# Eleven weight pieces subtracted on the pool engine, and x loaded over two queues, in a three-block fp32 kernel

## The chip, the cores and the metric

The kernel runs on one core of a Trainium2 chip. The metric is device time in microseconds (us) of one execution, the median of several runs. The engines are named as in the profile: PE is TensorE (matrix products), DVE is VectorE, ACT is ScalarE, POOL is GpSimd, and SP is SyncE, which here only issues transfers (DMAs). A DMA can be issued from the queue of SP, ACT or POOL.

## The reference

Three different blocks run one after the other on x, 512 tokens of 1,024 channels in fp32. Each one normalizes x, mixes tokens with two to four mixers, multiplies the merged result with an output matrix and adds it to x, normalizes again and adds an FFN. The first block, cut to this frame:

```python
def conv_glu_ffn(h, w_up, conv_w, w_down):
    u = causal_dwconv(h @ w_up.astype(h.dtype), conv_w)
    gate, up = jnp.split(u, 2, axis=-1)
    return (jax.nn.silu(gate) * up) @ w_down.astype(h.dtype)

def first_block(x, ...):
    ...
        h = rms_norm(x, mix_norm[l])
        z = h @ w_in[l].astype(h.dtype)
        ...
        merged = jnp.sum(gates.astype(ys.dtype) * ys, axis=2)
        x = x + merged @ w_o[l].astype(h.dtype)
        h2 = rms_norm(x, ffn_norm[l])
        x = x + conv_glu_ffn(h2, ffn_up[l], ffn_conv[l], ffn_down[l])
    return x

def reference(...):
    x = first_block(x, ...)
    x = second_block(x, ...)
    return third_block(x, ...)
```

The second block (gated delta rule and RWKV mixers) and the third (GLA and SSM mixers) have the same frame, with shift, scale and gate vectors from a condition (a "modulation").

## The kernel before

**Layout.** x lies as 8 tiles of 128 channels by 512 tokens. Work on x around a normalization is done in two halves of 256 tokens, so much of it has the shape 128x256. Weights are cut into blocks of 128x128; 8 blocks make a piece of 128x1024 fp32 (512 KB), and there are 464 pieces.

**Weights.** `load` (L319 to L331) issues the DMA of a raw piece `wr` from SP (L325), copies it on ACT to `wh` in a shorter form, fp32r (L328), and lets DVE form the rest `wl = wr - wh` (L329). Inputs are split the same way into `h` tiles. Each product then takes three matmuls: wh times high part, wh times low part, wl times high part (L358 to L360 in halves, L372 to L374 over all 512 tokens). `wr`, `wh` and `wl` have 3 buffers each, and `ahead` (L346) loads pieces up to two ahead of the one in use.

**Normalization.** `Rms.add` squares a tile of x on ACT (L495, L498 for the first tile) and adds the square to a sum (L496), on DVE, except for the second half of x at the start, where POOL adds. `stat` sums over channels with small matmuls on PE (L352, eight of them for a half). `mean` and `rsqrt` (L513 to L535) then do a chain of tiny 128x2 steps on DVE, each of which needs the one before it: shift and subtract, and three times L518, L520, L522. `factor` puts the result on a diagonal (L546, DVE) and spreads it over all partitions with one matmul (L548, PE). `into` multiplies x with it (L565, DVE), copies the high part on ACT (L569 or L572) and forms the low part on DVE (L570 or L573). These are the next products' inputs.

**Start.** `begin` (L758) issues the first half of x (8 tiles, L765), the first 256 columns of a constants table `con` (L205), the parameters `par` (L206), the second half of x, and then, in `constants`, the rest of `con` in five chunks (L213). Two constant tiles are copied to fp32r on ACT (L772): `onesr`, from the first 256 columns, and `bd64r`, whose source lies in the first of the five chunks.

**Ends.** `tail` (L816) does the output product of the mixers: five output tiles one by one, the last three (TAIL = 3) together in halves through `lins`, each added to x (L831); then the norm, the FFN, and x plus the FFN (L858, L860). In `ffn` the last output tile is made in halves (L475 to L480). At both ends the next product needs all of x, so the chain of adding, squares, `stat`, `rsqrt`, `factor` and `into` stands between two streams of matmuls.

**Order.** The code gives an order and priorities (`first`, which raises one); a scheduler then orders each engine's queue by priority and its own forecast of times. On the chip every engine works through its queue in that order and waits where an input is not there. `z.run` and `busy` weave background work in between; the change doesn't touch them.

Of the kernel before, what the change touches and what calls it, by code (L numbers as in the profile page):

```python
# [7 lines left out]
F32 = mybir.dt.float32  # L8
# [4 lines left out]
ALU = mybir.AluOpType  # L13
# [5 lines left out]
S = 512  # L19
# [166 lines left out]
class K:  # L186
# [78 lines left out]
                if next(g, self) is self:  # L265
                    gens.remove(g)

    busy = 0

    def tick(self):  # L270
        if not self.busy:
# [13 lines left out]
    def ada(self, which, c, ctx=False, chain=None):  # L285


        n = c.shape[2]
        s, th = [self.new([P, 8, n], tag="adas", bufs=2) for _ in range(2)]
        half = chain.t(8 * n).rearrange("p (k n) -> p k n", n=n)  # L290
        self.V.tensor_scalar(half, c, 0.5, None, op0=ALU.mult)
        self.A.activation(th, half, AF.Tanh)
        self.V.scalar_tensor_tensor(s, th, 1.0, half, op0=ALU.add, op1=ALU.mult)
        out = self.new([P, 64], tag="ada", bufs=1)
        self.ada_out = out
        yield
        for o in range(6):
            acc = [self.tile("ac", 1024) for _ in range(2 if ctx and o < 2 else 1)]
            for k in range(8):
                raw = self.tile("wa", 1024)  # L300
                at = ((which * 6 + o) * 8 + k) * 1024
                self.nc.sync.dma_start(raw, self.ap["wa"][:, at:at + 1024])
                for m, a in enumerate(acc):
                    if k:
                        self.V.scalar_tensor_tensor(a, raw, s[:, k, m:m + 1], a, op0=ALU.mult, op1=ALU.add)  # L305
                    else:
                        self.V.tensor_scalar(a, raw, s[:, k, m:m + 1], None, op0=ALU.mult)
                yield
            ps = self.bank("aux")
            for m, a in enumerate(acc):  # L310
                for b in range(8):
                    self.column(ps[:, 8 * m + b:8 * m + b + 1], a[:, b * P:b * P + P])
            self.V.tensor_copy(out[:, 8 * o:8 * o + 8], ps[:, :8])
            if len(acc) > 1:
                self.V.tensor_copy(out[:, 48 + 8 * o:56 + 8 * o], ps[:, 8:16])
            yield


    def load(self, n):  # L319
        n = min(n, self.ap["w"].shape[0])  # L320
        while self.loaded < n:
            i = self.loaded
            with self.first():
                raw = self.new([P, PIECE * P], F32, tag="wr", bufs=3)
                self.nc.sync.dma_start(raw, self.ap["w"][i])  # L325
                hi = self.new([P, PIECE * P], F32R, tag="wh", bufs=3)
                lo = self.new([P, PIECE * P], F32R, tag="wl", bufs=3)
                self.A.activation(hi, raw, AF.Copy)  # L328
                self.V.tensor_tensor(lo, raw, hi.bitcast(F32), op=ALU.subtract)  # L329
            self.pieces[i] = (hi, lo)  # L330
            self.loaded += 1  # L331

# [111 lines left out]
    def ffn(self, h, up, down, mid, out):  # L444


        m = {}

        def ups(a, b):
            for j in range(a, b):  # L450
                self.busy = 1 if j else self.busy
                if j % 11 == 0:
                    m[j // 11] = [], []
                if j > 1 or UP == 2 and j:
                    g, u = [self.lin(h, *w) for w in up(j)]
                elif j:
                    u = self.lin(h, *up(j)[1])
                    g = g1
                else:
                    (_, ps), _ = self.lins(h, *up(j), *(up(1)[:1] if UP > 2 else ()))  # L460
                    g, u = ps[:2]
                    g1 = ps[-1]
                self.split(m[j // 11], mid(j, g, u), lambda: self.tile("p", dt=F32R))

        ups(0, 11 + FFN_HEAD)
        for o in range(8):
            out(o, self.lin(m[0], down, P * o), slice(0, S))
            self.tick()
        ups(11 + FFN_HEAD, 22)
        for o in range(7):  # L470
            out(o, self.lin(m[1], down, P * o, 11 * P), slice(0, S), True)
            if o == 4:
                self.run(*self.bg)
                self.bg, self.busy = [], 0
        ps = self.bank("mm")  # L475
        w = self.take([(down, 11 * P + P * k, 7 * P) for k in range(11)])
        for n in HALVES:
            self.product(ps, w, m[1], n)
            out(7, ps, n, True)
        self.ahead()  # L480


class Rms:
# [260 lines left out]
def load_x(z, src, tag):  # L744
    X = [z.tile(tag) for _ in range(8)]
    for k in range(8):
        z.nc.gpsimd.dma_start(X[k], src[:, k * S:k * S + S])
    return X
# [9 lines left out]
def begin(z, src, which):  # L758

    with z.phase({"aux": 4}, x=8, f=8, wa=(2, 1024), ac=(3, 1024)):  # L760
        X = [z.tile("x") for _ in range(8)]
        for n in HALVES:
            with z.first((1 if n.start else 3) * HP):
                for k in range(8):
                    z.nc.sync.dma_start(X[k][:, n], src[:, k * S + n.start:k * S + n.stop])  # L765
                if n.start == 0:
                    z.parameters()
            if n.start == 0:
                z.load(1)
        z.constants()  # L770
        for x, y in ((z.onesr, z.ones), (z.bd64r, z.bd64)):
            z.A.activation(x, y, AF.Copy)  # L772
        c = Chain(z, "f", "aux")
        if which > 1:
            z.run(ada(z, which, c))
            modulation(z, which)
        r, h = Rms(c), z.rings()
        z.new([P, 96], tag="pad")
        a, b = HALVES
        for k in range(8):  # L780
            r.add(X[k], k, a)
        with z.first(2 * HP):
            by = r.of(r.mean(a))
            for k in range(8):
                r.add(X[k], k, b, z.G)
            by = r.into(h, X, *norm1(z, which), a, by, r.factor(lambda: r.mean(b)), 4)
            r.into(h, X, *norm1(z, which), b, by)
        return h


def norm1(z, which):
    return (z.q("mix_norm"), None) if which == 1 else (z.mod[:, 8:16], z.mod[:, 0:8])
# [8 lines left out]
def modulation(z, which):  # L801

    V = z.V
    mod = z.new([P, 64], tag=f"mod{which}")
    s = f"_{which}"
    V.tensor_tensor(mod[:, :48], z.ada_out[:, :48], z.q("b_ada" + s), op=ALU.add)
    if which == 3:
        V.tensor_tensor(mod[:, 48:], z.ada_out[:, 48:], z.q("b_ada" + s)[:, :16], op=ALU.add)
    for a, n in ((8, "norm1_w"), (32, "norm2_w"), (56, "norm1_w"))[:which]:
        V.scalar_tensor_tensor(mod[:, a:a + 8], mod[:, a:a + 8], 1.0, z.q(n + s), op0=ALU.add, op1=ALU.mult)  # L810
    for a in (16, 40)[:which - 1]:
        V.tensor_scalar(mod[:, a:a + 8], mod[:, a:a + 8], 0.5, None, op0=ALU.mult)
    z.mod = mod


def tail(z, m, src, dst, which, after):  # L816
# [3 lines left out]
    with z.phase({"aux": 4, "x": 1}, x=8, p=34, f=9, wa=(2, 1024), ac=(2, 1024)):  # L820
        c = Chain(z, "f", "aux")
        X = load_x(z, src, "x")
# [6 lines left out]
        def residual(o, ps, n):  # L829
            g = 0.5 if which == 1 else old[:, 16 + o:17 + o]  # L830
            V.scalar_tensor_tensor(X[o][:, n], ps[:, n], g, X[o][:, n], op0=mult, op1=add)  # L831
            r.add(X[o], o, n)

        w = "w_o" if which == 1 else "w_out" + s
        for o in range(8 - TAIL):
            residual(o, z.lin(m, w, P * o), slice(0, S))
        v = []
        for n, ps in z.lins(m, *((w, P * o) for o in range(8 - TAIL, 8))):
            with z.first(3 * HP):
                for e in range(TAIL):  # L840
                    residual(8 - TAIL + e, ps[e], n)
                v.append(r.mean(n))
                if not n.start:
                    by = r.of(v[0])
        with z.first(3 * HP):
            by = r.into(m, X, *norm, HALVES[0], by, r.factor(v[1]))
            r.into(m, X, *norm, HALVES[1], by)
        h = m

        own = {2: "norm_f_w_2", 3: "final_norm_w_3"}.get(which)  # L850
        r1 = Rms(c) if own else None
# [1251 lines left out]
def whole(z, out, blocks=(1, 2, 3)):  # L2103
    src = z.ap["x"]
    z.mod = None
    h = begin(z, src, blocks[0])
    for n, w in enumerate(blocks):
        m = (first, second, third)[w - 1](z, h)
        last = n == len(blocks) - 1
        dst = out if last else z.new([P, 8 * S], tag=f"x{w}", pool=z.dr)  # L2110
        h = tail(z, m, src, dst, w, None if last else w + 1)
        src = dst
# [20 lines left out]
```

## Time and profile before

| | us |
|---|---|
| median of 3 runs | 3309.65 |
| lowest and highest run | 3306.63, 3312.49 |
| the profiled execution | 3309.27 |
| its span (first to last instruction) | 3307.5 |
| PE busy in the span | 3217.7 (97%) |
| DVE, ACT, POOL busy | 67%, 45%, 3% |

How to read it: the span is what the trace covers; the profiled execution was 1.8 us longer than its span. A busy PE leaves some 90 us in which it does nothing. Those lie at the start and at a few seams between streams of matmuls. A timeline row gives the start in us, the time in us, the engine, the line, the operation with output and input, the shape, and how many instructions the row holds; in square brackets stands how long the engine was idle before, and what ended that wait.

### The profile page before, as it was taken

To read this page: it belongs to the slowest core of one execution; us is meant where nothing else is said; L and a number is where in the kernel's file an instruction comes from. 1 tells how busy PE (TensorE), PEld (TensorE's weight loads), DVE (VectorE), ACT (ScalarE), POOL (GpSimd) and SP (SyncE) were. 2 spreads that over 40 slices of the span, in tenths; PEclk is the share of its full clock that TensorE was granted. 3 is DMA by queue.
4 is the path that set the end of the run, shared out by engine and by line. 5 is a ranking of instruction groups with operands and counts; after the bars stand their busy time and mean duration, and the time that the engine had idled before them with its cause. 6 is when DMAs were issued, how large, how long until landed. Compare 5 with 4: busy or idle time off the path is not lost. (4 is left out here: it accounts for less than half of the span.)

```text
span 3307.5 us, 48313 instructions
## 1 busy us (share of the span) xinstructions
PE 3217.7 (97%) x19041; PEld 2671.8 (81%) x19041; DVE 2232.0 (67%) x3675; ACT 1496.2 (45%) x2493; POOL 101.5 (3%) x186
## 2 busy tenths in 40 slices
PE   7999999999999999999999999999999999999998
PEld 6778888888887787888888878888877778888887
DVE  5696646976577578666886568677688986453344
ACT  6542523433346657653432334645546665232222
POOL 0000000000000000000000001000010001000000
PEclk9999999999999999999999999999999999999999
DMA  4223333764332112215466324213227577423332
GB/s 135 71 71 102 92 124 96 229 203 148 109 101 72 52 39 83 79 43 181 136 208 224 96 82 134 73 64 98 84 87 233 174 218 234 128 90 96 96 97 76
DMA packets 128324, 393.33 MB, mean 119 GB/s; under 512 B 16056, under 2 KB 23480, under 8 KB 128096
## 3 DMA queue, kind: packets, MB, share of 16 engines
q1 hardware_dynamic: 113776, 346.82, 33.8%
q0 software_dynamic: 13168, 42.36, 3.7%
q8 instruction: 150, 2.46, 0.3%
q10 hardware_dynamic: 1152, 1.05, 0.1%
q14 instruction: 78, 0.64, 0.1%
HBM read 358.44 MB, written 31.74 MB: 118 GB/s over the span
## 5 line engine op out<-in xcount | busy, mean ns | idle before, releaser
L373 PE MATMUL mm<-h,wh 128*128 128x512 f32 x2400 | 948.2, 395 | 0.0
L372 PE MATMUL mm<-h,wh 128*128 128x512 f32 x2400 | 945.7, 394 | 1.6 <-ACT t L952 1.5
L374 PE MATMUL mm<-h,wl 128*128 128x512 f32 x2400 | 947.2, 395 | 0.0
L328 ACT ACTIVATE wh<-wr 128x1024 fp32r<-128x1024 f32 x464 | 490.5, 1059 | 935.9 <-PE mm L373 658.7
L329 DVE TENSOR_TENSOR wl<-wr,wh 128x1024 fp32r<-128x1024 f32 x464 | 567.2, 1223 | 459.6 <-ACT wh L328 453.8
L372 PEld LDWEIGHTS mm<-h,wh 128*128 128x128 f32 x2400 | 452.4, 188 | 98.1 <-issue 6.0
L374 PEld LDWEIGHTS mm<-h,wl 128*128 128x128 f32 x2400 | 452.1, 188 | 96.4 <-issue 4.5
L373 PEld LDWEIGHTS mm<-h,wh 128*128 128x128 f32 x2400 | 452.3, 188 | 95.0 <-issue 4.8
L373 PE MATMUL mm<-p,wh 128*128 128x512 f32 x599 | 233.4, 390 | 1.1 <-DVE p L434 1.1
L372 PE MATMUL mm<-p,wh 128*128 128x512 f32 x599 | 233.6, 390 | 0.0
L374 PE MATMUL mm<-p,wl 128*128 128x512 f32 x599 | 233.0, 389 | 0.0
L358 PE MATMUL mm<-h,wh 128*128 128x256 f32 (+1 forms) x480 | 158.5, 342 | 14.6 <-DVE t L1944 5.5
L359 PE MATMUL mm<-h,wh 128*128 128x256 f32 (+1 forms) x480 | 159.1, 337 | 0.6 <-DVE h L573 0.6
L360 PE MATMUL mm<-h,wl 128*128 128x256 f32 (+1 forms) x480 | 157.0, 332 | 0.0
L305 DVE SCALAR_TENSOR_TENSOR ac<-wa,adas,ac 128x1024 f32<-128x1024 f32 x98 | 125.3, 1280 | 24.4 <-DMA wa<-wa 23.9
L373 PEld LDWEIGHTS mm<-p,wh 128*128 128x128 f32 x599 | 112.4, 188 | 25.0 <-DVE p L434 1.7
L372 PEld LDWEIGHTS mm<-p,wh 128*128 128x128 f32 x599 | 112.4, 188 | 23.4
L374 PEld LDWEIGHTS mm<-p,wl 128*128 128x128 f32 x599 | 112.4, 188 | 23.4
L358 PEld LDWEIGHTS mm<-h,wh 128*128 128x128 f32 x480 | 91.2, 195 | 26.1 <-ACT h L572 5.1
L359 PEld LDWEIGHTS mm<-h,wh 128*128 128x128 f32 x480 | 93.4, 196 | 9.8 <-DVE h L573 2.0
L360 PEld LDWEIGHTS mm<-h,wl 128*128 128x128 f32 x480 | 93.4, 196 | 8.4
L754 DVE SCALAR_TENSOR_TENSOR f<-mm,par,f 128x511 f32<-128x511 f32 (+1 forms) x128 | 95.3, 745 | 1.1
(660 smaller groups left out, 5188.3 us busy)
## 6 DMA issues: line engine op xcount, KB each, us to landing
wr<-w SPq DMA_DIRECT2D x464, 512.0 KB, 3.6
wa<-wa SPq DMA_DIRECT2D x96, 512.0 KB, 4.3
e<-cum SPq DMA_DIRECT2D x64, 256.0 KB, 5.4
x<-x POOLq DMA_DIRECT2D x40, 256.0 KB, 5.1
s<-ecum SPq DMA_DIRECT2D x64, 128.0 KB, 4.7
cd<-t POOLq DMA_DIRECT2D x24, 256.0 KB, 2.3
gt<-t POOLq DMA_DIRECT2D x16, 256.0 KB, 2.5
fr<-gt SPq DMA_DIRECT2D x16, 256.0 KB, 2.9
```

The source lines that it names most:

```text
L305: self.V.scalar_tensor_tensor(a, raw, s[:, k, m:m + 1], a, op0=ALU.mult, op1=ALU.add)
L328: self.A.activation(hi, raw, AF.Copy)
L329: self.V.tensor_tensor(lo, raw, hi.bitcast(F32), op=ALU.subtract)
L358: self.T.matmul(ps[:, n], lhsT=wh, rhs=x[0][k][:, n], start=k == 0, stop=False)
L359: self.T.matmul(ps[:, n], lhsT=wh, rhs=x[1][k][:, n], start=False, stop=False)
L360: self.T.matmul(ps[:, n], lhsT=wl, rhs=x[0][k][:, n], start=False, stop=k == last)
L372: self.T.matmul(out, lhsT=wh, rhs=x[0][k], start=k == 0, stop=False)
L373: self.T.matmul(out, lhsT=wh, rhs=x[1][k], start=False, stop=False)
L374: self.T.matmul(out, lhsT=wl, rhs=x[0][k], start=False, stop=k == last)
L754: z.V.scalar_tensor_tensor(out[:, d:], src[:, :S - d], w[:, n - 1 - d:n - d], out[:, d:], op0=ALU.mult, op1=ALU.add)
```

## The change

Two things. First, a flag `edge` is set around the output product of the last three tiles of each mixer end up to and including the normalization behind it, and around the last product of each FFN. While it is set, `load` gives the subtraction of L329 to POOL (`self.G`) in place of DVE (`self.V`). `load` is called for 11 pieces there: three at each of the three mixer ends and one at each of the first two FFN ends (at the third FFN end no piece is left to load). The other 453 stay on DVE. Second, the 16 transfers of x in `begin` go alternately over the queues of SP (even tiles) and ACT (odd tiles), in both halves.

```diff
-    busy = 0
+    busy, edge = 0, False
...
                 self.A.activation(hi, raw, AF.Copy)
-                self.V.tensor_tensor(lo, raw, hi.bitcast(F32), op=ALU.subtract)
+                (self.G if self.edge else self.V).tensor_tensor(lo, raw, hi.bitcast(F32), op=ALU.subtract)
...
         ps = self.bank("mm")
+        self.edge = True
         w = self.take([(down, 11 * P + P * k, 7 * P) for k in range(11)])
         for n in HALVES:
             self.product(ps, w, m[1], n)
             out(7, ps, n, True)
         self.ahead()
+        self.edge = False
...
                 for k in range(8):
-                    z.nc.sync.dma_start(X[k][:, n], src[:, k * S + n.start:k * S + n.stop])
+                    (z.nc.sync, z.nc.scalar)[k % 2].dma_start(X[k][:, n], src[:, k * S + n.start:k * S + n.stop])
...
         v = []
+        z.edge = True
         for n, ps in z.lins(m, *((w, P * o) for o in range(8 - TAIL, 8))):
...
-        h = m
+        h, z.edge = m, False
```

The lines of the changed kernel have higher numbers: L496 becomes L498, L522 becomes L524, L548 becomes L550, L765 becomes L767, L772 becomes L774, L858 becomes L861.

The scheduler orders the queues anew. Three places matter.

The first is SP's queue at the start. `x6` to `x13` are the eight tiles of x, `con` the constants, `par` the parameters, `wr14` and `wr87` the first two raw weight pieces. Before:

```order
L765 DMA x6_73<-x 128x256
L765 DMA x7_74<-x 128x256
L765 DMA x8_75<-x 128x256
L765 DMA x9_76<-x 128x256
L765 DMA x10_77<-x 128x256
L765 DMA x11_78<-x 128x256
L765 DMA x12_79<-x 128x256
L765 DMA x13_80<-x 128x256
L205 DMA con2_64<-con 128x256
L206 DMA par1_63<-par 128x803
L765 DMA x6_73<-x 128x256
L325 DMA wr14_92<-w 128x1024
```

Now:

```order
L767 DMA x6_73<-x 128x256
L767 DMA x8_75<-x 128x256
L205 DMA con2_64<-con 128x256
L767 DMA x10_77<-x 128x256
L206 DMA par1_63<-par 128x803
L767 DMA x12_79<-x 128x256
L767 DMA x6_73<-x 128x256
L325 DMA wr14_92<-w 128x1024
L767 DMA x8_75<-x 128x256
L767 DMA x10_77<-x 128x256
L767 DMA x12_79<-x 128x256
L325 DMA wr87_321<-w 128x1024
```

SP has eight transfers of x fewer; the two halves of each odd tile stand in ACT's queue, one right behind the other, those of `x7`, `x9` and `x11` ahead of ACT's first computation and those of `x13` behind its first square.

The second place is ACT's queue later in the start. `f35` to `f41` are squares of the first half of x and `f48` to `f54` those of the second half, `wh` are weight pieces, `smga` is a small parameter tile. Before:

```order
L495 ACTIVATE f41_150<-x13_80 128x256
L772 ACTIVATE onesr3_65<-con2_64 128x128
L1198 ACTIVATE smga1407_7995<-par1_63 8x1
L498 ACTIVATE f17_113<-x6_73 128x256
L328 ACTIVATE wh15_94<-wr14_92 128x1024
L495 ACTIVATE f48_183<-x7_74 128x256
L495 ACTIVATE f49_186<-x8_75 128x256
L495 ACTIVATE f50_189<-x9_76 128x256
L495 ACTIVATE f51_192<-x10_77 128x256
L495 ACTIVATE f52_195<-x11_78 128x256
L495 ACTIVATE f53_198<-x12_79 128x256
L495 ACTIVATE f54_201<-x13_80 128x256
```

Now:

```order
L328 ACTIVATE wh15_94<-wr14_92 128x1024
L497 ACTIVATE f40_147<-x12_79 128x256
L497 ACTIVATE f41_150<-x13_80 128x256
L1201 ACTIVATE smga1407_7995<-par1_63 8x1
L328 ACTIVATE wh88_323<-wr87_321 128x1024
L328 ACTIVATE wh91_425<-wr90_423 128x1024
L774 ACTIVATE bd64r4_66<-con2_64 128x128
L497 ACTIVATE f48_183<-x7_74 128x256
L497 ACTIVATE f49_186<-x8_75 128x256
L497 ACTIVATE f50_189<-x9_76 128x256
L497 ACTIVATE f51_192<-x10_77 128x256
```

The second-half squares stand behind two more weight pieces (`wh88`, `wh91`), which before came only after them, and behind the copy to `bd64r`, which before stood far behind them, among the copies of L569.

The third place is the end of the first FFN. DVE's queue had the subtraction of the last product's loaded piece, `wl1357`, in the middle of the chain of `rsqrt` steps (`nw`) before:

```order
L518 SCALAR_TENSOR_TENSOR nw1349_7627<-nw1346_7615,nw1348_7626 128x2
L520 TENSOR_TENSOR nw1349_7627<-nw1349_7627,nw1348_7626 128x2
L522 SCALAR_TENSOR_TENSOR nw1348_7626<-nw1349_7627,nw1348_7626 128x2
L329 TENSOR_TENSOR wl1357_7695<-wr1355_7692,wh1356_7694 128x1024
L518 SCALAR_TENSOR_TENSOR nw1349_7627<-nw1346_7615,nw1348_7626 128x2
L520 TENSOR_TENSOR nw1349_7627<-nw1349_7627,nw1348_7626 128x2
L522 SCALAR_TENSOR_TENSOR nw1348_7626<-nw1349_7627,nw1348_7626 128x2
L518 SCALAR_TENSOR_TENSOR nw1349_7627<-nw1346_7615,nw1348_7626 128x2
L520 TENSOR_TENSOR nw1349_7627<-nw1349_7627,nw1348_7626 128x2
L522 SCALAR_TENSOR_TENSOR nw1348_7626<-nw1349_7627,nw1348_7626 128x2
L858 TENSOR_TENSOR x819_4241<-x819_4241,mm1343_7572 128x256
L546 TENSOR_SCALAR f1350_7639<-con2_64,nw1348_7626 128x128 x2
```

In the changed kernel that row is in POOL's queue, and the steps stand in a row in DVE's. On PE the matmul that spreads the factor (`aux1351`) has moved, here as a piece of the difference:

```order
 L360 MATMUL mm1343_7572<-p1285_7166,wl1336_7515 128x256
+L550 MATMUL aux1351_7642<-f1350_7639,con2_64 128x256
 L358 MATMUL mm1343_7572<-p1298_7244,wh1335_7514 128x256
 L359 MATMUL mm1343_7572<-p1299_7245,wh1335_7514 128x256
 L360 MATMUL mm1343_7572<-p1298_7244,wl1336_7515 128x256
-L548 MATMUL aux1351_7642<-f1350_7639,con2_64 128x256
 L352 MATMUL aux1354_7682<-con2_64,f891_4735 32x1 x8
```

It now stands three matmuls earlier, inside the last product (`mm1343`), so that the end of that product waits for it too. At the mixer ends of the second and third block the same matmul has moved nine matmuls forward; at the first mixer end it has not moved.

## Rows read from the trace of the kernel before

**Rows 1.** Busy time by stretch (us): span, then PE, PEld, DVE, ACT, POOL, clock, DMA share.

```profile
0.00:19.68 19.68, 1.93 (x34) 1.12 (x34) 10.57 (x37) 12.36 (x27) 6.33 (x11) 1.00 0.87 281
...
928.00:946.00 18.00, 14.32 (x124) 11.84 (x123) 14.72 (x52) 7.46 (x14) 0.54 (x1) 1.00 0.28 92
...
1950.00:1970.00 20.00, 15.67 (x157) 13.58 (x156) 17.26 (x74) 8.43 (x16) 0.00 (x0) 0.91 0.16 53
```

**Rows 2.** Timeline of PE at the start.

```profile
9.32 0.39 PE L352 MATMUL aux<-con,f 128*32 128x1 f32 x16 [9.32 <-DVE f L496]
...
19.36 0.39 PE L352 MATMUL aux<-con,f 128*32 128x1 f32 x16 [5.45 <-POOL f L496]
19.68 0.58 PE L358 MATMUL mm<-h,wh 128*128 128x256 f32 x1
```

**Rows 3.** Timeline of SP's queue at the start: issues of transfers.

```profile
0.75 3.71 SPq L765 DMA_DIRECT2D x<-x  x8
...
11.26 2.86 SPq L325 DMA_DIRECT2D wr<-w  x3
14.16 2.58 SPq L213 DMA_DIRECT2D con<-con  x5
```

**Rows 4.** Transfers issued up to 22 us: count, KB each, median us to landing.

```profile
con<-con SPq DMA_DIRECT2D x4, 256.0 KB, 6.0
```

**Rows 5.** Timeline of ACT at the start.

```profile
11.27 1.06 ACT L328 ACTIVATE wh<-wr 128x1024 fp32r<-128x1024 f32 x1 [1.10 <-DMA wr<-w]
12.23 1.93 ACT L495 ACTIVATE f<-x 128x256 f32<-128x256 f32 x6
...
21.14 0.29 ACT L772 ACTIVATE bd64r<-con 128x128 fp32r<-128x128 f32 x1
```

**Rows 6.** Timeline of POOL at the start, single instructions.

```profile
12.71 1.64 POOL L496 TENSOR_TENSOR f<-f,f 128x256 f32<-128x256 f32 x1 [12.26 <-ACT f L495]
...
16.04 0.73 POOL L496 TENSOR_TENSOR f<-f,f 128x256 f32<-128x256 f32 x1
```

**Rows 7.** Timeline of DVE at the start, beside those POOL instructions.

```profile
12.55 1.22 DVE L329 TENSOR_TENSOR wl<-wr,wh 128x1024 fp32r<-128x1024 f32 x1
...
16.39 0.66 DVE L570 TENSOR_TENSOR h<-f,h 128x256 fp32r<-128x256 f32 x1
...
19.90 0.42 DVE L570 TENSOR_TENSOR h<-f,h 128x256 fp32r<-128x256 f32 x1
```

**Rows 8.** Timelines of ACT, DVE and PE at the first FFN's end.

```profile
931.29 1.06 ACT L328 ACTIVATE wh<-wr 128x1024 fp32r<-128x1024 f32 x1 [0.90 <-PE mm L359]
...
932.50 0.16 DVE L522 SCALAR_TENSOR_TENSOR nw<-nw,nw 128x2 f32<-128x2 f32 x1
932.61 1.22 DVE L329 TENSOR_TENSOR wl<-wr,wh 128x1024 fp32r<-128x1024 f32 x1
...
935.13 0.48 DVE L546 TENSOR_SCALAR f<-con,nw 128x128 f32<-128x128 f32 x2
...
935.75 0.67 PE L548 MATMUL aux<-f,con 128*128 128x256 f32 x2 [1.15 <-DVE f L546]
937.77 0.31 PE L352 MATMUL aux<-con,f 128*32 128x1 f32 x16 [1.34 <-DVE f L496]
```

**Rows 9.** Timelines of ACT and DVE at the first mixer end.

```profile
561.01 1.06 ACT L328 ACTIVATE wh<-wr 128x1024 fp32r<-128x1024 f32 x1 [2.19 <-issue]
...
563.25 0.42 DVE L496 TENSOR_TENSOR f<-f,f 128x256 f32<-128x256 f32 x1
563.96 0.42 DVE L831 SCALAR_TENSOR_TENSOR x<-x,x 128x256 f32<-128x256 f32 x1 [0.29 <-PE x L360]
```

**Rows 10.** Timelines of ACT and DVE at the second mixer end.

```profile
1577.85 1.06 ACT L328 ACTIVATE wh<-wr 128x1024 fp32r<-128x1024 f32 x1 [2.29 <-PE mm L359]
...
1580.73 1.06 ACT L328 ACTIVATE wh<-wr 128x1024 fp32r<-128x1024 f32 x1 [1.51 <-issue]
...
1578.70 0.16 DVE L520 TENSOR_TENSOR nw<-nw,nw 128x2 f32<-128x2 f32 x1
...
1584.48 0.48 DVE L831 SCALAR_TENSOR_TENSOR x<-x,mod,x 128x256 f32<-128x256 f32 x1 [1.10 <-PE x L360]
```

## Prediction, made before the changed kernel was run

> **What bounds the kernel now.** I read the busy shares first, then the windows around the stretches where PE stands still, then the timelines there. PE works in nearly the whole span, so a cheaper DVE instruction is worth something only where PE waits for DVE. There are three kinds of such places. The first is the start: PE does 1.93 us of work in the first 19.68 us, while the DMA engines are 87% busy [rows 1]. The first product comes at 19.68, behind an L352 that waited 5.45 us for POOL's adds [rows 2]. So the second-half squares and adds set the start, not the first half, whose L352 was done at 9.32. The second kind is the FFN end: PE waits 1.15 us for DVE's L546 and then 1.34 us for L496 [rows 8]. The third is the mixer end, where the last add to x (L831) waits for PE, and not PE for it [rows 9, 10]; PE only waits behind that add, for the norm that follows it.
>
> **The start.** The change takes eight issues off SP. One costs 3.71 / 8 = 0.46 us [rows 3], and the raw piece wr14 is now eighth in SP's queue and was twelfth: it is issued up to 4 x 0.46 = 1.9 us sooner, or no sooner where SP waits for something else. What decides, however, is ACT's new order. There the copy to bd64r stands ahead of all second-half squares. Its source is the first constants chunk, which SP issues right behind three weight transfers, at 14.16 [rows 3]. The third of these comes only after DVE has subtracted the first piece, which ended at 12.55 + 1.22 = 13.77 [rows 7]. The chunk therefore moves with wr14: issue at 12.3 to 14.2. Such a chunk took 6.0 us to land [rows 4], so it is there at 18.3 to 20.2, and with 0.29 us for the copy [rows 5] the squares begin at 18.6 to 20.5; before they began at 12.23 [rows 5]. From there to the L352 it was 19.36 - 12.23 = 7.1 us [rows 2, 5], in which one of the seven adds took 1.64 us and an undisturbed one takes 0.73 [rows 6]. Seven of the latter and a square of some 0.4 us make 5.5 us. The L352 lands at 24.1 to 27.6 where it was at 19.36: **4.7 to 8.3 us later**. I take 5.0, near the early end, since less is queued ahead of the chunk than before. The copy cost nothing before because it ran at 21.14 [rows 5], after the squares; that cover is gone. ACT's own issues of x delay its squares too, by about 0.46 us each, but this lies ahead of the wait for the chunk and adds nothing. What is late next are POOL's adds and, behind the squares on ACT, the copies of L571.
>
> The Trainium skill (DMA: Bandwidth & Descriptors, section Issuing engines are not separate DMA queues) says that transfers issued from several engines run on the same 16 DMA engines, and that the gain is only the sequencer's issue time. By that rule the two queues give at most the 1.9 us above, with the order of the engines unchanged; the 87% agrees with it.
>
> **The FFN ends.** 11 subtractions leave DVE; 453 stay. POOL's time for a 128x1024 subtraction isn't in the trace. Its 128x256 add takes 0.73 us [rows 6]: four times that is 2.9 us, the upper end. DVE went from 0.42 us at 256 [rows 7] to 1.22 at 1024, a factor of 2.9, which gives 2.1 us, the lower end. I take 2.4, since part of 0.73 must be a fixed cost. The other question is what DVE can do meanwhile. At the start POOL's first add took 1.64 us in place of 0.73 while DVE's L329 ran [rows 6, 7], and a DVE L570 took 0.66 in place of 0.42 beside a POOL add that began at 16.04 [rows 6, 7]. In both pairs the later one ended only after the earlier had let go. All of these have two SBUF inputs, as the subtraction and the rsqrt steps have. I read this as a **lock**: while POOL subtracts, such DVE steps stand still.
>
> The Trainium skill (SBUF — State Buffer, section Who interferes with whom) states it as a rule: DVE's second port pair is shared with GpSimd under an exclusive lock. The two pairs agree in size. Without that rule the sum would be the first rival's.
>
> At the first FFN end wh is done at 931.29 + 1.06 = 932.35 [rows 8]. POOL then holds the lock to 934.45 to 935.25 (taken: 934.75). DVE's L522, at 932.50 before, waits for that. From L522 to L546 it was 935.13 - 932.50 = 2.63 us [rows 8], of which about 1.14 was the subtraction and 0.33 the add L858, now behind L546; 1.16 us are left. L546 begins at 935.6 to 936.4 (935.9) and L550, 0.62 us behind as before (935.75 - 935.13), at 936.2 to 937.0. But L550 now stands three matmuls ahead of the product's end, so PE holds the end back: some 0.9 us for it (0.67 before) and those three, then the add to x, a square and the add of the square at 0.4 us each with hand-overs, together 1.4 us. L352 comes at 938.5 to 939.3 where it was at 937.77: 0.7 to 1.5 later, I take **+1.1**. The second FFN end has the same pattern, so 2.2 us for both (1.4 to 3.0). Behind POOL's instruction in its own queue stands one store of x, for which nobody waits soon.
>
> **The mixer ends.** At the first, wh is done at 561.01 + 1.06 = 562.07, POOL holds to 564.2 to 565.0 (564.5). L496, which has two SBUF inputs, ran at 563.25 and the last L831 at 563.96 [rows 9]. Now L496 ends at 564.6 to 565.4 and L831 follows: +0.65 to +1.45, I take 0.95. At the second end wh is done at 1580.73 + 1.06 = 1581.79, POOL holds to 1583.9 to 1584.7, L496 ends at 1584.3 to 1585.1, and L831 was at 1584.48 [rows 10]: 0 to +0.6, I take 0.15, and the same at the third end; together 0.3 (0 to 1.2). The DVE time set free gains nothing here, since L831 waited for PE already (1.10 us there).
>
> **Clock.** Around the second FFN end the granted clock was 0.91 in 20 us [rows 1], which is 0.09 x 20 = 1.8 us of TensorE time lost at the half level. Longer waits at the seams can bring one more such spell, or none: 0 to 1.8, I take 0.9.
>
> **Sum.** 5.0 + 2.2 + 0.95 + 0.3 + 0.9 = 9.35 us. The profiled execution took 3309.27, 1.8 above its span of 3307.5; it would take 3318.6 with a span of 3316.9. The median of the runs is 0.4 above the profiled one, so **3319.0**. The lower bounds make 6.75, the upper 15.75: 3316 to 3325.
>
> **Rivals.**
> (a) No lock: POOL and DVE run side by side, or the instructions miss each other. For it speaks that the pairs above are few. Then the start costs 5.0, and each FFN end gains: L546 at 935.13 - 1.14 - 0.33 = 933.66, before the product's end, and the two waits of 1.15 and 1.34 shrink to one of 1.3: -1.2 each. Mixer ends 0. Total +2.6: 3312.3, within the measurement. Chance 0.20.
> (b) The other side, **the start gains**: the chunk lands before the squares would be due, so that the copy ahead of them costs nothing. It decides at about 12 us, when the squares began before; the chunk would have to be issued at about 6, while three weight pieces stand ahead of it. Then the first product is up to 1.9 us sooner, and with the FFN gains of (a) the time is 3309.65 - 1.9 - 2.4 = 3305.3, and below 3303 if the seams also lose one low-clock spell (1.8). Against it: the 13.77 of the first subtraction, which needs a piece landed behind all x. Chance 0.12.
> (c) The rsqrt chain is caught at the second and third mixer end as well. Its step L522 is free to start at 1578.70 + 0.16 plus a hand-over, about 1578.90, and the first of the three pieces' wh is done at 1577.85 + 1.06 = 1578.91 [rows 10]: a margin near nothing. If POOL gets in first, the chain stops for POOL's whole 2.1 to 2.9 us, and PE with it, since L550 has moved nine matmuls forward into the stream. Price 2.5 each, 5.0 in all: 3324, with one more low-clock spell 3326. Chance 0.13.
>
> **How the numbers follow.** The forecast has 0.55. About 0.2% (6.6 us) is what a measurement can tell from no change: below 3303.0 is faster, above 3316.3 slower. Faster: 0.06 from (b), 0.02 from (a), 0.08. Within: 0.15 from (a), 0.06 from (b), 0.03 from the forecast's lower edge, 0.24. Slower: 0.52 from the forecast, 0.13 from (c), 0.03 from (a) with a dearer start, 0.68. The range takes in (c) and most of (a): 3311 to 3327; left out are (b), 0.12, and some 0.03 below and 0.04 above.
>
> **What the new profile should show.** bd64r's copy on ACT (L774) at 18 to 21 us, with a wait for the DMA of con ahead of it; the first product at 24 to 26; eleven POOL subtractions of 2.1 to 2.9 us; beside them a DVE step of 128x2 that takes some 2 us in place of 0.16 at both FFN ends, and an L550 for which PE waits more than 1.15 us. At mixer ends the L498 beside POOL should be long. A first product before 20 us would refute the start; DVE steps of 0.16 us beside a running POOL subtraction would refute the lock and leave (a).

## The result, and the profile after

The changed kernel took 3330.82 us (median of 6 runs, 3329.84 to 3336.29), the kernel before 3310.69 in the same comparison: a ratio of 1.0063 (95% interval 1.0053 to 1.0073), 20.1 us **slower**. The prediction was 3319.0 with a range of 3311 to 3327. The direction was right; the size was half of what came, and the time lies outside the range.

The page of the changed kernel, its first lines (busy us, share of the span, instructions):

```profile
span 3330.6 us, 48328 instructions
...
PE 3223.5 (97%) x19041; PEld 2679.5 (80%) x19041; DVE 2241.6 (67%) x3664; ACT 1496.6 (45%) x2493; POOL 126.8 (4%) x197
```

The profiled execution took 3332.39 us, with a span 23.1 us longer than before (3330.6 against 3307.5); the medians differ by 20.1. PE has the same 19041 matmul records and is busy 5.8 us longer (3223.5 against 3217.7): the same matmuls ran slower in places. The other 17.3 us are waiting. Three places hold nearly all of it.

**The start.** Timelines of PE and ACT, as in [rows 2, 5]:

```profile
14.46 0.39 PE L352 MATMUL aux<-con,f 128*32 128x1 f32 x16 [14.46 <-DVE f L498]
...
24.94 0.39 PE L352 MATMUL aux<-con,f 128*32 128x1 f32 x16 [1.77 <-POOL f L498]
25.26 0.79 PE L358 MATMUL mm<-h,wh 128*128 128x256 f32 x2
...
4.65 1.28 ACT L500 ACT_TABLE_LOAD   x1 [4.65 <-DMA x<-x]
...
18.59 0.31 ACT L774 ACTIVATE bd64r<-con 128x128 fp32r<-128x128 f32 x1 [1.03 <-DMA con<-con]
18.80 2.23 ACT L497 ACTIVATE f<-x 128x256 f32<-128x256 f32 x7
23.81 1.20 ACT L571 ACTIVATE h<-f 128x256 fp32r<-128x256 f32 x3 [2.77 <-DVE f L567]
```

The first product starts at 25.26 where it was at 19.68: 5.6 us later. The second-half squares stand behind bd64r's copy, as the order said, and the L352 behind them comes at 24.94; this chain ends last. But the first half is late too: its L352 comes at 14.46, before at 9.32, and its first input to the products (L571) is copied at 23.81, before (L569) at 14.71. That copy ends some 1 us ahead of the first product, so freeing the second half alone could bring about that much. PE makes up 1.2 of the 5.6 us soon behind the first product: its 128x256 matmuls take 0.41 us at first and 0.28 from 28.1 on, where before they did so from 25.5 on, only 2.6 sooner. From there the stream runs 4.4 us late.

**A mixer end.** Timelines of DVE, POOL and PE at the first one, as in [rows 9]. On DVE, L548 is the pair of instructions that was L546 before, which puts the factor on a diagonal; L550 is PE's matmul behind it:

```profile
562.86 2.57 DVE L548 TENSOR_SCALAR f<-con,nw 128x128 f32<-128x128 f32 x2
...
568.85 2.41 DVE L498 TENSOR_TENSOR f<-f,f 128x256 f32<-128x256 f32 x1 [0.90 <-ACT f L497]
...
562.95 2.40 POOL L329 TENSOR_TENSOR wl<-wr,wh 128x1024 fp32r<-128x1024 f32 x1 [9.78 <-ACT wh L328]
568.60 2.39 POOL L329 TENSOR_TENSOR wl<-wr,wh 128x1024 fp32r<-128x1024 f32 x1 [3.25 <-ACT wh L328]
...
565.49 0.70 PE L550 MATMUL aux<-f,con 128*128 128x256 f32 x2 [2.09 <-DVE f L548]
```

L548, a pair that took 0.48 us before [rows 8], takes 2.57 and ends only when POOL's subtraction ends. L550 stands in the stream of PE's products, so PE waits 2.09 us in the middle of it. This is the second of the three POOL subtractions at this end. The third catches L498 (2.41 us), and the norm behind the stream comes later. What PE waited for in this stretch (us in total, times, longest):

```profile
PE mm L358 <- ACT h L571: 2.1, 1, 2.1
PE aux L550 <- DVE f L548: 2.1, 1, 2.1
```

4.2 us, where before it was one wait of 1.7. At the second and third mixer end it is the same: 4.4 and 4.3 us against 1.8 each. The three lose 7.6 us together, of which 6.2 are the new wait for L548 (2.1, 2.1 and 2.0).

**An FFN end.** Timelines of DVE, POOL and PE at the first one, as in [rows 8]:

```profile
940.12 2.38 DVE L524 SCALAR_TENSOR_TENSOR nw<-nw,nw 128x2 f32<-128x2 f32 x1
...
940.10 2.38 POOL L329 TENSOR_TENSOR wl<-wr,wh 128x1024 fp32r<-128x1024 f32 x1 [5.40 <-ACT wh L328]
...
944.34 0.67 PE L550 MATMUL aux<-f,con 128*128 128x256 f32 x2 [2.46 <-DVE f L548]
...
947.30 0.39 PE L352 MATMUL aux<-con,f 128*32 128x1 f32 x16 [1.94 <-DVE f L498]
```

The forecast step, a 128x2 instruction of over 2 us in place of 0.16, is there. At the second FFN end the step beside POOL has a single input:

```profile
1968.53 2.32 DVE L515 TENSOR_SCALAR nw<-nw 128x2 int32<-128x2 int32 x1
```

PE's waits from the last product to the norm's products rise from 3.7 to 5.3 us at the first FFN end and from 4.4 to 5.7 at the second. The three places make 5.6 + 7.6 + 2.9 = 16.1 of the 17.3 us of waiting.

**The clock.** Busy time by stretch behind the two FFN ends, as in [rows 1] (the column before the DMA share is the granted clock):

```profile
936.00:950.00 14.00, 9.09 (x88) 8.33 (x87) 9.58 (x31) 4.77 (x8) 2.94 (x2) 0.87 0.19 59
...
1966.00:1984.00 18.00, 12.92 (x126) 11.63 (x127) 14.93 (x63) 6.72 (x12) 2.40 (x1) 0.72 0.20 60
```

0.87 and 0.72, where the stretches of [rows 1] had 1.00 and 0.91: more of them ran at the half level (1.2 of 2.4 GHz). That the longer waits brought this is not shown. The last run of the start below, which has no POOL subtraction and the waits of before at its FFN ends, shows 0.88 at the first, over the same work:

```profile
928.00:942.00 14.00, 11.00 (x101) 10.09 (x100) 11.33 (x41) 5.89 (x10) 0.54 (x1) 0.88 0.35 109
```

Matched matmul by matmul with the trace before, the slower matmuls cost 4.8 us in the five stretches of 500 matmuls that hold the seams (0.6 to 1.3 in each) and 2.5 in two stretches without a seam; the start gives 1.3 back. The clock also differs from run to run: the trace before is of a run with a mean clock of 0.995, where the kernel's runs averaged 0.9933, and the trace of the changed kernel of one with 0.990, where its runs averaged 0.9917. In runs of the kernel before a mean clock lower by 0.001 went with some 2 us (9 runs at 0.992 averaged 3313.1, 41 at 0.993 3310.8, 24 at 0.994 3309.1). By this some 3 of the 20 us go with the lower clock.

### The profile page after: what moved, and what is told of

Its sections match the earlier page's. It is cut to its first block, busy times and chain, and to the rows that moved or that the text cites. A ratio compares the mean times of both kernels' runs of the same rounds, so it can differ in the third digit from the quotient of the medians.

```text
span 3330.6 us, 48328 instructions
## 1 busy us (share of the span) xinstructions
PE 3223.5 (97%) x19041; PEld 2679.5 (80%) x19041; DVE 2241.6 (67%) x3664; ACT 1496.6 (45%) x2493; POOL 126.8 (4%) x197
## 4 chain that ended last, share of the span: by engine, by line
PE 69%; issue 19%; DVE 6%; ACT 3%; POOL 1%; DMA 1%; SPq 0%; POOLq 0%; DVEq 0%; ACTq 0%
PE mm L372 18%; PE mm L373 18%; PE mm L374 18%; PE mm L358 1%; PE mm L359 1%; PE mm L360 1%; DVE wl L329 1%; PE r L661 1%; ACT wh L328 1%; PE g L661 1%; PE g L713 1%; PE r L720 1%; PE r L713 1%; DMA x<-ob 1%; PE g L720 1%
## 5 line engine op out<-in xcount | busy, mean ns | idle before, releaser
L329 DVE TENSOR_TENSOR wl<-wr,wh 128x1024 fp32r<-128x1024 f32 x453 | 553.7, 1223 | 460.6 <-ACT wh L328 455.2
```

The costliest lines, as they stand in the source:

```text
L329: (self.G if self.edge else self.V).tensor_tensor(lo, raw, hi.bitcast(F32), op=ALU.subtract)
```

## The experiments

Ratios are to the kernel before, measured beside each (3309.8 to 3310.9 us). Line numbers differ a little from run to run: the pair L546 is L547 in the runs of the start and L550 in the run with four parts, and the step L522 is L523 to L526.

**The two parts alone.** The loading of x alone (flag never set):

```diff
-        self.edge = True
...
-        z.edge = True
```

> Only the two-queue loading of x; the flag edge is never set, so all 464 subtractions stay on DVE. My theory: the two parts add up, and the start alone costs what the changed kernel lost up to 60 us in its trace, 4 to 5 us: some 3315, with the first product at about 25.3 us and waits of 1.15 us for L546 at the FFN ends as before. Rival: the late start is absorbed at the next waits, and the time is that of the kernel before, 3311.

Measured: 3318.19 us, 1.0024 (1.0014 to 1.0034), +7.9; the first product at 25.8 us, 6.1 later than before. The subtractions alone (x over SP):

```diff
-                    (z.nc.sync, z.nc.scalar)[k % 2].dma_start(X[k][:, n], src[:, k * S + n.start:k * S + n.stop])
+                    z.nc.sync.dma_start(X[k][:, n], src[:, k * S + n.start:k * S + n.stop])
```

> Only the subtractions on POOL; x comes over SP's queue alone. My theory (a lock between POOL's subtraction and DVE): first product at 19.7 us, DVE steps of over 2 us beside each of the POOL subtractions that meets a norm, and 15 to 16 us over the kernel before: 3326. Rival (the seams only suffered because the late start shifted the schedule against the DMAs): under 3318.

Measured: 3323.05 us, 1.0046 (1.0034 to 1.0059), +12.7. The two make 20.6 together, the whole change 20.1: they add up within their intervals, and the rivals (absorbed, or shifted) fall. I had expected 4 to 5 and 15 to 16: the start is dearer, the seams cheaper. Of the 7.9, the 1.8 beyond the late first product go with a lower mean clock in these runs (0.9924 against 0.9935).

**What a POOL subtraction holds.** The blocks are left out; each form of DVE instruction runs beside a POOL subtraction, then alone:

```diff
+            A.activation(a[:, :256], d, AF.Copy)
+            G.tensor_tensor(g, a, X[:, 1024:2048], op=sub)
+            A.activation(b, a[:, :256], AF.Copy)
+            one(f, b, p, e)      # tensor_tensor, tensor_scalar, copy, ...
```

> The three blocks are left out; in their place one POOL subtraction of 128x1024 after another, each with one DVE instruction of 128x256 (or 128x2) that is started while POOL runs, and the same DVE instruction again while POOL is idle. Theory A, on which the prediction rested: only instructions with two inputs in SBUF are held (tensor_tensor and scalar_tensor_tensor, L2120, L2130, L2138): about 1 to 2 us in place of 0.16 to 0.45; tensor_scalar, copies and casts run as when alone. Theory B: whatever DVE reads and writes in SBUF alone is held, tensor_scalar and copies too (L2124, L2126, L2134, L2136, L2140), and only instructions with an input in PSUM run freely (L2122, L2128, L2132).

DVE's timeline of this run; of each pair the first (u...) was started beside POOL, the second (v...) alone; `pp` lies in PSUM, where the results of PE lie too; the other tiles lie in SBUF, as x and the weights do. Then two of POOL's instructions, beside L2122 and L2128:

```profile
16.38 0.42 DVE L2122 TENSOR_TENSOR uttp<-pp,xx 128x256 f32<-128x256 f32 x1 [2.63 <-ACT pp L2155]
18.22 0.42 DVE L2122 TENSOR_TENSOR vttp<-pp,xx 128x256 f32<-128x256 f32 x1 [1.42 <-ACT pp L2159]
...
27.79 0.42 DVE L2128 TENSOR_SCALAR utsp<-pp 128x256 f32<-128x256 f32 x1 [1.35 <-ACT pp L2155]
...
31.56 2.22 DVE L2130 SCALAR_TENSOR_TENSOR ustt<-bstt,xx 128x256 f32<-128x256 f32 x1 [0.93 <-ACT bstt L2152]
...
39.58 2.08 DVE L2134 COPY ucp<-bcp 128x256 f32<-128x256 f32 x1 [0.93 <-ACT bcp L2152]
42.00 0.29 DVE L2134 COPY vcp<-bcp 128x256 f32<-128x256 f32 x1 [0.33 <-ACT bcp L2157]
...
50.37 1.96 DVE L2140 TENSOR_SCALAR uts<-bts 128x2 f32<-128x2 f32 x1 [0.93 <-ACT bts L2152]
52.79 0.17 DVE L2140 TENSOR_SCALAR vts<-bts 128x2 f32<-128x2 f32 x1 [0.46 <-ACT bts L2157]
...
57.72 2.15 DVE L2124 TENSOR_SCALAR uts<-bts 128x256 f32<-128x256 f32 x1 [0.93 <-ACT bts L2152]
60.21 0.29 DVE L2124 TENSOR_SCALAR vts<-bts 128x256 f32<-128x256 f32 x1 [0.33 <-ACT bts L2157]
...
14.38 2.35 POOL L2151 TENSOR_TENSOR gttp<-attp,xx 128x1024 f32<-128x1024 f32 x1 [1.56 <-ACT attp L2150]
...
26.96 2.34 POOL L2151 TENSOR_TENSOR gtsp<-atsp,xx 128x1024 f32<-128x1024 f32 x1 [1.36 <-ACT atsp L2150]
```

Theory A falls, B holds for the forms tried. A tensor_scalar or a copy with a single input in SBUF is held as long as an instruction with two (0.29 becomes 2.1), at 128x2 as at 128x256; the three forms tried with an input in PSUM run beside POOL at their own speed (0.42, and 0.48 for scalar_tensor_tensor). POOL, which came first each time, is not slowed.

**The lock, by length.** In these three runs x comes over SP. POOL's subtraction twice:

```diff
-                (self.G if self.edge else self.V).tensor_tensor(lo, raw, hi.bitcast(F32), op=ALU.subtract)
+                for _ in range(2 if self.edge else 1):
+                    (self.G if self.edge else self.V).tensor_tensor(lo, raw, hi.bitcast(F32), op=ALU.subtract)
```

> As the run with the edge part alone (3323.1), but each of the eleven POOL subtractions is done twice, one behind the other; the order of the other engines is unchanged. Lock theory: at the three mixer ends two steps each (L548's successor and the add of the squares) and at the two FFN ends one step each stand some 2.4 us longer, 8 x 2.4 = 19 us, less what other waits cover: 3337 to 3342. Rival (the cost came from the moved order of PE, POOL's own length plays no part): 3323 to 3326.

Measured: 3332.31 us, 1.0063 (1.0047 to 1.008), +9.3 on the edge part alone: more than the rival allows (the interval begins at 3326), less than the 14 to 19 that I expected. The first FFN end, DVE and then POOL, shows why:

```profile
937.00 2.38 DVE L525 SCALAR_TENSOR_TENSOR nw<-nw,nw 128x2 f32<-128x2 f32 x1
939.41 0.16 DVE L521 SCALAR_TENSOR_TENSOR nw<-nw,nw 128x2 f32<-128x2 f32 x1
939.61 2.19 DVE L523 TENSOR_TENSOR nw<-nw,nw 128x2 f32<-128x2 f32 x1
...
936.99 4.80 POOL L330 TENSOR_TENSOR wl<-wr,wh 128x1024 fp32r<-128x1024 f32 x2 [5.40 <-ACT wh L328]
```

A waiting DVE step gets in between the two POOL instructions. A chain of steps pays for both, a single step only for one. POOL subtracting 256 columns only, the other 768 copied unsubtracted by ACT:

```diff
...
+                if self.edge:
+                    self.G.tensor_tensor(lo[:, :256], raw[:, :256], hi[:, :256].bitcast(F32), op=ALU.subtract)
+                    self.A.activation(lo[:, 256:], raw[:, 256:], AF.Copy)
+                else:
+                    self.V.tensor_tensor(lo, raw, hi.bitcast(F32), op=ALU.subtract)
```

> As the run with the edge part alone (3323.1), but POOL subtracts only 256 of the 1024 columns of each of the eleven pieces; the other 768 are copied unsubtracted by ACT (the subtraction of those columns is left out). PE's matmul that spreads the factor stands as far forward as in the changed kernel. Lock theory: POOL holds DVE for 0.7 us in place of 2.4, so most of the 12.7 us goes: 3311 to 3315. Rival (moved order): 3320 to 3324 as before.

Measured: 3313.59 us, 1.0011 (1.0001 to 1.002), +2.9. The order on PE was that of the changed kernel, so 9.8 of the 12.7 us go by the length of POOL's instruction, and at most the other 2.9 by the moved order. All columns on POOL, in four instructions:

```diff
...
+                for j in range(0, PIECE * P, 256) if self.edge else (None,):
+                    q = slice(None) if j is None else slice(j, j + 256)
+                    (self.V if j is None else self.G).tensor_tensor(lo[:, q], raw[:, q], hi[:, q].bitcast(F32), op=ALU.subtract)
```

> As the run with the edge part alone (3323.1), but each of the eleven POOL subtractions is done in four instructions of 256 columns. The order on PE is unchanged. Theory (the lock belongs to one instruction and a waiting DVE step gets in between two of POOL's): a single DVE step that meets POOL waits 0.7 us in place of 2.4, so the mixer ends lose 1 to 1.7 us less at each of two places; the chain at the FFN ends, where one step follows the other, waits for each of the four parts and stays as it was: 3315 to 3319. Rival (POOL holds DVE off until its queue is empty): 3323 to 3326, with DVE steps of 2.4 us or more.

Measured: 3316.55 us, 1.0026 (1.0016 to 1.0035), +6.7. DVE's timeline at the first mixer end (first row) and, from its third step on, through the chain at the first FFN end:

```profile
558.30 0.96 DVE L550 TENSOR_SCALAR f<-con,nw 128x128 f32<-128x128 f32 x2
...
933.38 0.73 DVE L526 SCALAR_TENSOR_TENSOR nw<-nw,nw 128x2 f32<-128x2 f32 x1
934.15 0.66 DVE L522 SCALAR_TENSOR_TENSOR nw<-nw,nw 128x2 f32<-128x2 f32 x1
934.85 0.65 DVE L524 TENSOR_TENSOR nw<-nw,nw 128x2 f32<-128x2 f32 x1
935.53 0.65 DVE L526 SCALAR_TENSOR_TENSOR nw<-nw,nw 128x2 f32<-128x2 f32 x1
```

The mixer ends recover (0.96 for the pair in place of 2.57), and the FFN chain waits for each of the four parts: these four steps take 2.8 us in place of 0.8. POOL's whole queue does not hold DVE off; one instruction does.

**The FFN ends alone.**

```diff
-        z.edge = True
```

> The flag edge is set at the two FFN ends only (2 subtractions on POOL), x over SP alone. Theory (each seam costs its own waits and low-clock spells, independent of the others): 5 of the 12.7 us, 3315. Rival (the cost lies at the mixer ends; the FFN ends gain what the freed DVE time gives, 1.1 us each): 3308 to 3311.

Measured: 3315.13 us, 1.0013 (1.0004 to 1.0022), +4.5. So the two FFN ends have 4.5 of the 12.7 us, which leaves 8.2 for the three mixer ends; these were not run alone. The rival falls: what DVE was freed of does not outweigh the waits.

**The start, taken apart.** First, bd64r's source put into the first chunk of the constants, so that its copy waits for nothing late (x over both queues, all on DVE):

```diff
-        self.nc.sync.dma_start(self.con[:, :256], self.ap["con"][:, :256])
+        self.nc.sync.dma_start(self.con[:, :384], self.ap["con"][:, :384])
...
-        for a in range(256, self.c.n, 512):
+        for a in range(384, self.c.n, 512):
```

> As the run with x over two queues alone (3318.2), but the first chunk of the constants is 384 columns wide in place of 256, so that bd64r's source comes with it and its copy no longer waits for the late chunk (it now stands ahead of ACT's first square). Theory on record in the prediction (the copy's wait decides the start): first product near 20 to 21 us, 3313. Theory from the trace of the changed kernel (the copy waited only 1.0 us for its chunk; the two weight pieces ahead of the squares and the first half's late chain do the rest): first product at 24 to 25 us, 3316 to 3318.

Measured: 3320.30 us, 1.0029 (1.0018 to 1.004): no better than 3318.2. Timelines of PE and ACT:

```profile
16.54 0.40 PE L352 MATMUL aux<-con,f 128*32 128x1 f32 x16 [16.54 <-DVE f L497]
25.36 1.22 PE L549 MATMUL aux<-f,con 128*128 128x256 f32 x2 [8.43 <-DVE f L547]
27.67 0.58 PE L358 MATMUL mm<-h,wh 128*128 128x256 f32 x1 [0.77 <-ACT h L570]
...
0.74 6.69 ACTq L766 DMA_DIRECT2D x<-x  x8
7.46 1.28 ACT L773 ACT_TABLE_LOAD   x1 [7.46 <-DMA x<-x]
```

The copy was free of its wait, and the first product came later still, at 27.67: both forecasts missed. The squares of the second half gained 1.4 us (17.86, with x over two queues alone 19.27). But the run moved more than the copy: all eight issues on ACT now stand ahead of its first computation, and its table load comes at 7.46 in place of 4.66. Here L549 of the first half is the late one: from its L352 to it 8.8 us, in the kernel before 3.4 (9.32 to 12.69). So the copy's wait alone does not explain the start; how much it costs when all else stays is not shown. Second, the first half of x over two queues, the second half over SP:

```diff
-                    (z.nc.sync, z.nc.scalar)[k % 2].dma_start(...)
+                    (z.nc.sync, z.nc.scalar if n.start == 0 else z.nc.sync)[k % 2].dma_start(...)
```

> All subtractions on DVE; the first half of x alternates between the queues of SP and ACT, the second half comes over SP alone. ACT's queue keeps the second-half squares ahead of the second and third weight piece and of the copy to bd64r. My theory (ACT's order sets the start): first product at 18 to 20 us, 3309 to 3311. Rival (the issues on ACT themselves and the mixed queues delay the first half): first product at 22 us or later, 3313 or more.

Measured: 3313.93 us, 1.0012 (1.0003 to 1.0021), first product at 20.8 us. ACT's order is nearly that of before, and it still loses: the first product lies between the two forecasts, the time in the rival's. ACT's and DVE's timelines:

```profile
0.74 1.86 ACTq L766 DMA_DIRECT2D x<-x  x4
2.63 1.28 ACT L499 ACT_TABLE_LOAD   x1 [2.63 <-issue]
...
14.24 0.68 DVE L523 SCALAR_TENSOR_TENSOR nw<-nw,nw 128x2 f32<-128x2 f32 x1
14.95 0.16 DVE L519 SCALAR_TENSOR_TENSOR nw<-nw,nw 128x2 f32<-128x2 f32 x1
15.15 0.58 DVE L521 TENSOR_TENSOR nw<-nw,nw 128x2 f32<-128x2 f32 x1
```

ACT issues four transfers before it does anything else, so its table load ends at 3.9 us where it ended at 2.0. The first half's L352 comes at 11.2, and its rsqrt chain now runs beside POOL's adds: every other step waits 0.6 us. In the kernel before this chain was through as the adds began (L548 at 12.69, POOL's first add at 12.71). That this is the same lock is what the next run tries. Third, then, the adds of the second half on DVE in place of POOL, in this kernel, in the one with both halves over two queues, and in the kernel before:

```diff
-                r.add(X[k], k, b, z.G)
+                r.add(X[k], k, b)
```

> As the run with the first half of x over two queues (first product at 20.8 us, 3313.9), but the second-half adds on DVE. Lock theory (there the rsqrt chain of the first half ran beside POOL's adds, its steps taking 0.6 us in place of 0.16): the chain from L532 to L547 takes some 3.8 us with one subtraction inside it, in place of 6.7; first product at 18 to 19 us, 3309 to 3312. Rival (the chain was late for other reasons): first product at 20.5 us or later, 3313 or more.

Measured: 3312.36 us, 1.0006 (0.9997 to 1.0015). L547 is done in time for L549 at 15.5 in place of 18.5, and the first product comes at 18.2: the chain is as the lock theory has it. The two times (3312.4 and 3313.9) lie too close together to tell.

> As the run with both halves over two queues alone (first product at 25.8 us, 3318.2), but the second-half adds on DVE. Theory: the part of the late start that comes from POOL's adds goes (0.75 us each against 0.35, and the held steps), the part from the late first half (first L352 at 15 us in place of 9.3) and from the weight subtractions inside the chain stays: first product at 22 to 23.5 us, 3315. Rival (only the adds were at fault): 20 us, 3312; rival (only the late first half): 25 us, 3318.

Measured: 3316.11 us, 1.0015 (1.0006 to 1.0025), first product at 23.9 us. That is 1.9 sooner than with the adds on POOL. The first product now waits for the first half alone (1.54 us for ACT's L570), since L352 still comes at 14.9 and two weight subtractions still stand in the chain.

> The kernel before, but the seven second-half adds at the start (L496) are done by DVE, not POOL, so that no POOL instruction works there. Lock theory: nothing changes for the first half's rsqrt chain, which was over at 12.6 us before POOL began; the adds take 0.35 us each in place of 0.75, the second L352 comes at 16 to 17.5 us in place of 19.4, the first product then waits for its input at 17 to 18: 3308 to 3310. Rival (DVE is the bottleneck of the start): first product no earlier than 19.7, 3311.

Measured: 3311.09 us, 1.0000 (0.9992 to 1.0009). PE's timeline of this last one:

```profile
16.72 0.58 PE L358 MATMUL mm<-h,wh 128*128 128x256 f32 x1 [2.67 <-ACT h L569]
...
18.39 0.39 PE L352 MATMUL aux<-con,f 128*32 128x1 f32 x16
18.71 0.58 PE L358 MATMUL mm<-h,wh 128*128 128x256 f32 x1
```

The first product comes 3 us sooner, as forecast, but the stream behind it starts at 18.7, 1 us sooner, and the median shows nothing of it. No version tried beats the kernel before.

## Why the prediction failed

- **What bounds the kernel** held: the loss lies at the start and the five seams, and the middle of the blocks adds little.
- **POOL's time** was taken as 2.4 us between 2.1 and 2.9; the eleven took 2.35 to 2.40.
- **The mixer ends** were taken as 0.95 + 0.15 + 0.15; they were 2.5, 2.6 and 2.5. This is the term that broke the range, and the step that failed is the reading of the lock: "All of these have two SBUF inputs, as the subtraction and the rsqrt steps have". L546 (now L548) is a tensor_scalar with one input, and its meeting with POOL stood in the sum at nothing. The run of forms shows that it is held just as long (2.1 in place of 0.29), and PE's wait for it makes 6.2 of the 7.6 us. The Trainium skill (SBUF — State Buffer, section Who interferes with whom) says this as well: copy, cast and tensor_scalar in their two-port modes contend too. I used only the half of the rule that my two rows showed. At all three ends the second POOL subtraction began within 0.2 us of L548's start and held it, with PE behind it. The L498 part came as written, 2.41 us beside POOL, and the wait behind it grew by 0.4 to 0.5 at each end. Rival (c) had this place, its price (2.5) and the near-zero margin, but through another step and without the first mixer end: its 3324 to 3326 came nearer by luck.
- **The start** was taken as 5.0 us; the first product was 5.6 late, and loading x over two queues cost 7.9 by itself. The chain that was forecast is in the trace: squares at 18.80 (18.6 to 20.5), L352 at 24.94 (24.1 to 27.6). The copy itself waited only 1.03 us for its chunk; the two weight pieces ahead of it had waited 2.4 already. What failed is "not the first half", and that ACT's own issues add nothing. Six issues of x and their waits hold ACT's table load back to 4.65 us, L352 of the first half is 5.1 us late, its chain then holds two weight subtractions and meets POOL's adds. So both halves are late, within some 1 us of each other, and with the second half out of the way the first product still came only at 23.9. The rule of the Trainium skill (DMA: Bandwidth & Descriptors, section Issuing engines are not separate DMA queues) that several engines save only the issue time agrees, in that nothing was won. What the ACT queue pays for the issues is shown by the table load here.
- **The FFN ends** were taken as +1.1 each, 2.2 in all; in the run with them alone they cost 4.5. The steps (a 128x2 step of over 2 us, L550 inside the product) came as written, and the late end of the product behind L550 as well. At the first end the whole stream ran 7.6 us late already, so L550 at 944.34 is 936.7 in the times of before, inside the forecast (936.2 to 937.0); but L352 behind it came 1.9 later than before, not 0.7 to 1.5. The 1.4 us from the product's end to L352 was too short: ACT copied a weight piece (945.33, 1.06 us) ahead of the square. At the second end, where L550 had moved by one matmul only, the matmuls between ran at the half level (L550 took 1.03 in place of 0.67).
- **The clock** was taken as 0.9 us; the slower matmuls are 5.8 us in the profiled execution and some 3 in the median. I allowed one more spell for six changed places. What brings a spell was not tried and stays open, as do the 1.2 us of waiting outside the three places.
- **The other rivals**: (a), no lock, is refuted by the run of forms; (b), a start that gains, by the loading of x alone.

With the mixer ends at 7.6 and the clock at 3, the sum of the prediction (5.0 + 2.2) would have been 17.8 us, and 3327. The 2.3 that the FFN ends were dearer in their own run are as much as is left of the 20.1, though they hold some of the clock's share too.

## What to carry to other kernels

Moving work to POOL does not free DVE where both read SBUF: while one of POOL's tensor_tensor instructions ran, every form of DVE instruction tried here that has its tensors in SBUF alone stood still, a 128x2 one as long as a 128x256 one. Put POOL's work where DVE has only PSUM work or none, ask of each chain of tiny steps what POOL does beside it, and if it can't be avoided, cut POOL's instruction into short ones, which helps a lone step but not a chain. A transfer issued from a computing engine's queue costs that engine's own first work (ACT's table load at 4.65 us in place of 0.74); and a chain that just misses a collision in the trace of before can meet it when it is moved by a microsecond or two.

## What the runs showed that was not expected

- A tensor_scalar, copy or cast with its one input in SBUF is held by POOL (1.96 to 2.15 us in place of 0.17 to 0.29); a tensor_scalar with that input in PSUM takes 0.42 beside POOL and alone.
- The lock passes between instructions: a DVE step got in between two POOL instructions that stood back to back (2.38, then 0.16, then 2.19 us). Four POOL instructions of 256 columns took 2.8 to 3.3 us together in place of 2.4 for one of 1024.
- Slower matmuls made up a quarter of the loss in the profiled execution (5.8 of 23.1 us), most of it at the seams; that the longer waits bring the half level is not shown.
